# A written order for VectorE and ScalarE through the second half's short heads

## The chip, the cores and the metric

The kernel runs on one core of a Trainium2 chip. A core has a matrix engine (TensorE, PE in the profile; its weight loads are listed as PEld), an elementwise engine (VectorE, DVE), an engine for activation functions and casts (ScalarE, ACT), a general engine (GpSimd, POOL), which here mostly issues transfers, and SyncE (SP), which issues the other transfers. Each engine works through its own list of instructions in the order in which the list was built; semaphores hold an instruction until what it needs is there. The metric is the device time of one execution, in microseconds. Lower is better.

## The reference

One layer of a decoder trunk on a sequence of 1024 tokens with a model width of 2048, all in 32-bit floats:

```python
hn = rmsnorm(h, norm_mix_g[i])
proj = hn @ w_in[i]
sb_q, sb_k, sb_v, sb_g, df_q, df_k, df_v, df_g = jnp.split(proj, split_at, axis=-1)
sb_out = stick_breaking_attention(sb_q, sb_k, sb_v)          # 8 heads of 128
df_out = differential_attention(rope(df_q), rope(df_k), df_v, lam)   # 8 heads, two score maps each
df_out = rmsnorm(df_out, subln_g[i]) * (1.0 - lambda_init)
mixed = concat([sb_out * silu(sb_g), df_out * silu(df_g)])
h = h + mixed @ w_out[i]
gate = sigmoid(rmsnorm(h, norm_ple_g[i]) @ w_ple_gate[i])
h = h + gate * (p[i] @ w_ple_proj[i])
out = rmsnorm(h, norm_final_g)
```

In a stick-breaking head the weight of key s for query t is `sigmoid(z_ts)` times the product of `1 - sigmoid(z_tj)` over all j between s and t. The kernel forms that product with a scan along the keys. A differential head subtracts `lam` times a second softmax from a first one, and its output goes through a norm of its own.

## The kernel before, in words

**Three products for one.** A 32-bit product is made of three: each operand is split into a high part (a cast on ScalarE) and a low part (the rest, a subtraction on VectorE), and TensorE multiplies high by high, high by low and low by high. So nearly every tile that goes into a product costs one ScalarE instruction and one VectorE instruction first. The names end in `h` or `hi` and `l` or `lo`: `whi` and `wlo` for input weights (L149, L150), `awh` and `awl` for transposed attention weights (L375, L376).

**Halves and heads.** The tokens are worked in two halves of 512, half 1 first and then half 0. In each half come the eight differential heads (numbers 8 to 15) and then the eight stick-breaking heads (0 to 7), here called short heads, since only q and k are projected for them: their v and gate come from a stage before, by a transfer from `vg_d`. In half 0 the keys and values of half 1 are read back too (`k2`, `v2`), so a row block of 128 queries has up to 1024 keys there.

**Units and ticks.** The projection of a head is a `unit`: four pieces of weights, each two column groups of four steps. A step is three matmuls of 128 x 512 (L219 to L221), followed by one tick of a counter, `side.tick()`. A short head has one unit, 32 ticks; a differential head has two. The attention of a head does not run by itself: after its unit, `attention` returns a list of steps with tick offsets, and `side.add` mixes them into the ticks of the units that follow. So TensorE alternates between the projection of one head and the attention of the head before it. A step of offset t runs at tick t + 1. Head 7's steps run in the output stage's first products (`product(..., tick=True)`).

**The steps of a short head.** `weights(rb, c)` for the four row blocks: the scores `z` on TensorE, the causal mask (L304) on VectorE, two sigmoids (L318, L319) on ScalarE, the scan (L320) and a product (L321) on VectorE. `values` transposes v. `turn(pr, g)` transposes the weights of a pair of row blocks, and `parts` splits what comes out. `mix(pr, g)` multiplies by v (L391 to L396), and after the last group the result is summed (L401, L402), multiplied by the gate and written out by `mixed`, with transfers from SyncE (`mixed_d`, some `comb_d`) and from GpSimd (`comb_d`, added to what is there). A differential head has a softmax in place of the scan (maximum L325, exponential L328), and a norm behind its mix (`norm`, roots at L91 and L92, step at L93 to L95 and L426).

**What sets the order.** TensorE's list follows the program text throughout (`manual_schedule` over TensorE). VectorE's and ScalarE's lists follow the text only in a stage before the heads and in a part of the output stage; through the heads, the build's scheduler puts them in order. When a step runs, all of its instructions are issued at that point of the text: `weights` issues scores, mask, sigmoids, scan and product together, and the scheduler decides where they stand among the others. The eviction of q and k after a unit (L1018 to L1021) and the gate with `vf` and `gf` (L1046 to L1055) are issued directly after the unit.

**Buffers that matter here.** `z` and the transposes are in PSUM. `sg`, which holds the gate and then the output of a head, has three buffers; `sm` and `sqv` share five, `bt` has three, `qz` two. ScalarE's functions come in table sets, and where consecutive functions belong to different sets, an `ACT_TABLE_LOAD` stands between them.

Of the kernel before, what the change touches and what calls it, by code (L numbers as in the profile page):

```python
# [20 lines left out]
P = 128  # L21
# [14 lines left out]
SECOND = 16, 12  # L36
# [12 lines left out]
def _body(ctx, nc, tc, ap):  # L49
# [93 lines left out]
    def wprep(wsrc, pc, by_halves=False, later=False):  # L143
# [44 lines left out]
    class Side:  # L188

        def __init__(self):  # L190
            self.q = []
            self.now = 0

# [74 lines left out]
    def attention(at, pz, half, hd, q, qz, K, KL, VV, sg, vf):  # L268
# [10 lines left out]
        def scores(c, rb):  # L279
# [19 lines left out]
            mask = masks[:, 0 if sb else 1, :]  # L299
            if rb == 3:  # L300
                zm = ev.tile([P, P], F32, name="zm", tag="zm", bufs=1)
                V.tensor_tensor(zm, z[:, 2 * P:3 * P], mask, op=ALU.add)
                mask = zm
            V.tensor_tensor(z[:, rs], z[:, rs], mask, op=ALU.add)  # L304
            return z

        def weights(rb, c):
            off = rb * P
            vw = slice(off, nkey)
            z = scores(c, rb)  # L310
            if sb:
                pt = at.tile([P, S], F32, name="pt", tag="pt")
                if rb == 2:
                    bt = at.tile([P, S], F32, name="bt2", tag="qz")
                else:
                    bt = at.tile([P, S], F32, name="bt", tag="bt", bufs=3)
                st = at.tile([P, S], F32, name="st", tag="st")
                A.activation(pt[:, vw], z[:, vw], AF.Sigmoid, scale=-SB_SCALE)  # L318
                lastsig[0] = A.activation(bt[:, vw], z[:, vw], AF.Sigmoid, scale=SB_SCALE)  # L319
                V.tensor_tensor_scan(st[:, off + 1:nkey], pt[:, off:nkey - 1], pt[:, off:nkey - 1], initial=1.0, op0=ALU.mult, op1=ALU.bypass)  # L320
                V.tensor_tensor(bt[:, off + 1:nkey], st[:, off + 1:nkey], bt[:, off + 1:nkey], op=ALU.mult)  # L321
                ws[rb] = bt
                return
            mx = at.tile([P, 1], F32, name="mx", tag="mx", bufs=8)
            V.reduce_max(mx, z[:, vw], axis=AX.X, negate=True)  # L325
            et = at.tile([P, S], F32, name="et", tag="pt" if c else "bt", bufs=2 if c else 3)
            l = at.tile([P, 1], F32, name="l", tag="l", bufs=8)
            A.activation(et[:, vw], z[:, vw], AF.Exp, bias=mx[:, 0:1], accum_out=l)  # L328
            V.reciprocal(l, l)
            if c == 0:  # L330
                es[rb] = et, l
                return
            e0, r0 = es[rb]
            V.tensor_tensor(l, l, lam, op=ALU.mult)
            A.activation(et[:, vw], et[:, vw], AF.Copy, scale=l[:, 0:1])
            V.scalar_tensor_tensor(e0[:, vw], e0[:, vw], r0[:, 0:1], et[:, vw], op0=ALU.mult, op1=ALU.subtract)
            ws[rb] = e0

        def values():
# [5 lines left out]
            A.copy(v[:, 0], vps)  # L345
            V.tensor_tensor(v[:, 1], vps, v[:, 0].bitcast(F32), op=ALU.subtract)
            if half == 1:
                G.dma_start(v_d[hd], v.rearrange("p a b c -> p (a b c)"))
# [16 lines left out]
        def parts(pr, g, tp, wh, wl):  # L365
            if g == 0:
                lead = at.tile([P, 2, P], F32R, name="lead", tag="lead")
                A.copy(lead[:, 0], tp[:, 0, 0:P])
                V.tensor_tensor(lead[:, 1], tp[:, 0, 0:P], lead[:, 0].bitcast(F32), op=ALU.subtract)
                wjs[pr, g] = [lead, (wh[:, 1, :], wl[:, 1, :])]  # L370
                o = slice(1, 2)
            else:
                wjs[pr, g] = [(wh[:, j, :], wl[:, j, :]) for j in range(2)]
                o = slice(0, 2)
            A.copy(wh[:, o, :], tp[:, o, :])  # L375
            V.tensor_tensor(wl[:, o, :], tp[:, o, :], wh[:, o, :].bitcast(F32), op=ALU.subtract)  # L376

        def mix(pr, g):
# [22 lines left out]
            A.copy(sm[:, 1, :], av4[:, 3, :])  # L401
            V.reduce_sum(sm[:, 0, :], av4[:, 0:3, :].rearrange("p a b -> p b a"), axis=AX.X)  # L402
            av = sm.rearrange("p a b -> p (a b)")
            if sb:
                V.tensor_tensor(sg[:, ms_], av, sg[:, ms_], op=ALU.mult)
                if pr == 1:
                    mixed(half, hd, sg)
                return
            sq = ev.tile([P, 2 * P], F32, name="sqv", tag="sm", bufs=5)
            A.activation(sq, av, AF.Square)  # L410
            V.scalar_tensor_tensor(sg[:, ms_], av, subg[:, 0:1], sg[:, ms_], op0=ALU.mult, op1=ALU.mult)
            sqh = ev.tile([P, 2 * P], F32R, name="sqh", tag="sm", bufs=5)
            sql = ev.tile([P, 2 * P], F32R, name="sql", tag="sm", bufs=5)
            A.copy(sqh, sq)
            V.tensor_tensor(sql, sq, sqh.bitcast(F32), op=ALU.subtract)
            sqs[pr] = sq, sqh, sql

        def norm(pr):
# [6 lines left out]
            rstd_from(msq, 1.0, eps5, SUB_EPS, rs_, sq)  # L425
            V.tensor_tensor(sg[:, ms_], sg[:, ms_], rs_, op=ALU.mult)  # L426
            if pr == 1:
                mixed(half, hd, sg)
# [4 lines left out]
        if sb:  # L433
            b = 12 if hd == 0 else 6
            ss, t0 = [[b], [b + 3], [b + 7], [b + 11]], b + 16
            t1 = t0 + SECOND[half]
        else:
            tight = hd == 2 * H - 1
# [5 lines left out]
            t1 = s3[-1] + (13 if tight else LATD[half])  # L444
        steps = [(t, partial(weights, rb, c)) for rb, ts in enumerate(ss) for c, t in enumerate(ts)]
        steps.append((t0 - 2 if sb else ss[1][-1] + 2, values))
        for pr, t, n in ((0, t0, n0), (1, t1, n1)):
# [4 lines left out]
            steps.append((t + gap * n + (2 if sb and pr else 0), partial(mix, pr, n - 1)))  # L452
# [4 lines left out]
    with tc.tile_pool(name="at", bufs=2) as at, tc.tile_pool(name="pz", bufs=2, space=PSUM) as pz:  # L457
# [510 lines left out]
        for half in (1, 0):  # L968
# [15 lines left out]
            for hd in (ORDER0, ORDER1)[half]:  # L984
# [15 lines left out]
                acc = unit(X, mid={2: load_vg} if sb else None)  # L1000
                rstd = rstds[half]
                q = at.tile([P, 2, HALF], F32R, name="q", tag="q")
                k = at.tile([P, 2, HALF + P], F32R, name="k", tag="k")
# [9 lines left out]
                for c, t in ((0, q), (1, k)):  # L1013
                    f = f32t("qk")
                    if c == 0 and not sb:
# [3 lines left out]
                    if sb:  # L1019
                        A.copy(t[:, 0, :HALF], f)  # L1020
                        V.tensor_tensor(t[:, 1, :HALF], f, t[:, 0, :HALF].bitcast(F32), op=ALU.subtract)  # L1021
                        continue
# [23 lines left out]
                V.tensor_tensor(vf, vacc[0], rstd, op=ALU.mult)  # L1046
                V.tensor_tensor(gf, vacc[1], rstd, op=ALU.mult)
                sg = at.tile([P, HALF], F32, name="sg", tag="sg", bufs=3)
                if 0 < hd < H or (half == 0 and hd == H):
                    lastsig[0] = A.activation(sg, gf, AF.Sigmoid)  # L1050
                else:
# [518 lines left out]
```

## Time and profile before

| what | value |
| --- | --- |
| median of 3 runs | 2515.66 us (2514.49 to 2515.76) |
| profiled execution: its time, its span | 2515.73 us, 2514.0 us |
| mean granted TensorE clock | 0.991 |
| TensorE busy | 2421.5 us |
| VectorE busy | 1792.6 us |
| ScalarE busy | 1215.5 us |
| GpSimd busy | 279.6 us |
| moved by DMA | 397.72 MB |

Half 1's short heads lie at about 765 to 1060 us of the span, half 0's differential heads at 1060 to 1425, and half 0's short heads at 1425 to 1739, each unit some 36 to 38 us long but for the third, of 54 us. The output stage follows.

In the rows below, an engine's busy time counts its instructions without waiting. In a timeline row come the start, the duration, the engine, the line, the operation, output <- inputs and the tile sizes; in brackets stands how long the engine stood idle before it, and the instruction whose end released it. A matmul's duration holds its latency: what counts is the distance to the next start.

### The profile page before, as it was taken

What the parts mean: (1) busy time and instruction counts of PE and PEld (TensorE: products, weight loads), DVE (VectorE), ACT (ScalarE), POOL (GpSimd) and SP (SyncE); (2) the same over time, 40 slices, a digit from 0 to 9 for tenths busy, and PEclk for the clock granted to TensorE, in tenths of its full rate; (3) what the DMA queues carried; (4) which work ended last, traced back from release to release, by engine and by line L of the source; (5) the groups of instructions that cost most, each with busy time, mean ns of one, the idle gap of its engine ahead of it and who ended that gap; (6) DMA issues with size and microseconds to landing.
All of it is one profiled execution on the core that took longest, in us unless ns stands there. A gap on an engine that the chain in (4) does not pass through costs nothing.

```text
span 2514.0 us, 31908 instructions
## 1 busy us (share of the span) xinstructions
PE 2421.5 (96%) x11434; PEld 2005.8 (80%) x11434; DVE 1792.6 (71%) x3010; ACT 1215.5 (48%) x2067; POOL 279.6 (11%) x361
## 2 busy tenths in 40 slices
PE   8999999999999999999999988998899999999997
PEld 6787878888888887888888877887787887787886
DVE  6888777777777768688888876778577674546554
ACT  5233345555555445555566654445423224546433
POOL 1211110000000001000000000110111112330110
PEclk9999999999999999999999999999999999999998
DMA  8777654544354556343434344546746777343333
GB/s 292 255 263 223 214 193 143 164 130 151 122 153 145 168 176 186 107 113 106 122 114 122 110 122 97 143 124 186 232 162 213 169 189 230 110 137 104 131 109 101
DMA packets 167472, 397.72 MB, mean 158 GB/s; under 512 B 18897, under 2 KB 23249, under 8 KB 167313
## 3 DMA queue, kind: packets, MB, share of 16 engines
q1 hardware_dynamic: 131040, 302.07, 37.6%
q0 software_dynamic: 36272, 93.60, 14.4%
q8 instruction: 90, 1.47, 0.2%
q14 instruction: 70, 0.57, 0.1%
HBM read 297.03 MB, written 106.95 MB: 161 GB/s over the span
## 4 chain that ended last, share of the span: by engine, by line
PE 79%; DVE 10%; DMA 5%; ACT 4%; issue 3%; SPq 0%; DVEq 0%; POOL 0%; ACTq 0%
PE acc L219 16%; PE acc L220 16%; PE acc L221 16%; PE pbc L518 4%; PE pbc L516 4%; PE pbc L517 4%; PE tp L359 2%; DVE st L320 2%; PE pa L518 1%; PE pa L516 1%; PE pa L517 1%; PE av L396 1%; PE z L297 1%; PE z L298 1%; PE av L395 1%
## 5 line engine op out<-in xcount | busy, mean ns | idle before, releaser
L219 PE MATMUL acc<-xh,whi 128*128 128x512 f32 x1568 | 629.3, 401 | 1.5 <-DVE gt L1183 1.5
L221 PE MATMUL acc<-xh,wlo 128*128 128x512 f32 x1568 | 613.9, 392 | 0.0
L220 PE MATMUL acc<-xl,whi 128*128 128x512 f32 x1568 | 613.8, 391 | 0.0
L150 DVE TENSOR_TENSOR wlo<-wraw,whi 128x1024 fp32r<-128x1024 f32 x252 | 312.6, 1240 | 243.0 <-ACT whi L149 236.5
L149 ACT CAST whi<-wraw 128x1024 fp32r<-128x1024 f32 x252 | 264.9, 1051 | 295.5 <-PE acc L220 264.3
L221 PEld LDWEIGHTS acc<-xh,wlo 128*128 128x128 f32 x1568 | 295.5, 188 | 64.8
L219 PEld LDWEIGHTS acc<-xh,whi 128*128 128x128 f32 x1568 | 296.0, 189 | 57.2 <-issue 2.4
L220 PEld LDWEIGHTS acc<-xl,whi 128*128 128x128 f32 x1568 | 296.5, 189 | 54.7 <-issue 0.5
L606 ACT CAST wpr<-T 128x512 fp32r<-128x512 f32 x128 | 78.0, 621 | 317.4 <-DVE T L564 313.1
L375 ACT CAST awh<-tp 128x256 fp32r<-128x256 f32 (+1 forms) x160 | 80.1, 501 | 150.2 <-PE tp L359 124.8
L376 DVE TENSOR_TENSOR awl<-tp,awh 128x256 fp32r<-128x256 f32 (+1 forms) x160 | 92.8, 580 | 65.3 <-ACT awh L375 63.7
L328 ACT ACTIVATE et<-z,mx 128x512 f32<-128x512 f32 (+7 forms) x128 | 94.5, 738 | 51.1 <-DVE mx L325 49.5
L111 POOL TENSOR_TENSOR ssq<-ssq,sq 128x512 f32<-128x512 f32 x56 | 83.6, 1494 | 304.8 <-ACT sq L110 254.1
L320 DVE TENSOR_TENSOR_SCAN st<-pt 128x511 f32<-128x511 f32 (+3 forms) x64 | 86.5, 1352 | 23.8 <-ACT pt L318 23.8
L325 DVE TENSOR_REDUCE mx<-z 128x1 f32<-128x512 f32 (+7 forms) x128 | 96.4, 753 | 1.2
L620 DVE TENSOR_TENSOR wpr<-T,wpr 128x512 fp32r<-128x512 f32 x128 | 87.7, 685 | 5.8 <-ACT wpr L606 3.9
L396 PE MATMUL av<-awl,v 128*128 128x256 f32 x256 | 76.1, 297 | 16.0 <-DVE awl L376 15.9
L516 PE MATMUL pbc<-cS,wpr 128*128 128x512 f32 x224 | 87.4, 390 | 3.2 <-DVE u L1327 1.6
L517 PE MATMUL pbc<-cS,wpr 128*128 128x512 f32 x224 | 87.2, 389 | 0.0
L518 PE MATMUL pbc<-cS,wpr 128*128 128x512 f32 x224 | 87.2, 389 | 0.0
L318 ACT ACTIVATE pt<-z 128x512 f32<-128x512 f32 (+3 forms) x64 | 41.6, 651 | 81.6 <-DVE z L304 80.4
L394 PE MATMUL av<-awh,v 128*128 128x256 f32 x256 | 72.8, 284 | 5.5 <-ACT awh L375 5.5
(399 smaller groups left out, 5354.2 us busy)
## 6 DMA issues: line engine op xcount, KB each, us to landing
wraw<-w_in SPq DMA_DIRECT2D x192, 512.0 KB, 3.6
wraw<-w_gate SPq DMA_DIRECT2D x64, 512.0 KB, 3.6
wraw<-w_out SPq DMA_DIRECT2D x72, 256.0 KB, 3.6
wraw<-w_vg SPq DMA_DIRECT2D x71, 256.0 KB, 4.2
comb_d<-sg POOLq DMA_DIRECT2D x48, 256.0 KB, 7.5
spare<-xT SPq DMA_DIRECT2D x44, 256.0 KB, 4.2
xl<-h_d SPq DMA_DIRECT2D x40, 256.0 KB, 4.3
vghalf_d<-hc POOLq DMA_DIRECT2D x32, 256.0 KB, 4.1
```

Source lines behind the costliest of these rows:

```text
L149: A.copy(hi[:, o], raw[:, o])
L150: V.tensor_tensor(lo[:, o], raw[:, o], hi[:, o].bitcast(F32), op=ALU.subtract)
L219: T.matmul(acc[c], hi[:, k2, kh, c, :], xh, start=first, stop=False)
L220: T.matmul(acc[c], hi[:, k2, kh, c, :], xl, start=False, stop=False)
L221: T.matmul(acc[c], lo[:, k2, kh, c, :], xh, start=False, stop=last)
L320: V.tensor_tensor_scan(st[:, off + 1:nkey], pt[:, off:nkey - 1], pt[:, off:nkey - 1], initial=1.0, op0=ALU.mult, op1=ALU.bypass)
L325: V.reduce_max(mx, z[:, vw], axis=AX.X, negate=True)
L328: A.activation(et[:, vw], z[:, vw], AF.Exp, bias=mx[:, 0:1], accum_out=l)
L396: T.matmul(av, vv[:, 0, blk % 4, :], wl, start=False, stop=last)
L516: T.matmul(o, wh[:, w], xh, start=start and k == 0, stop=False, skip_group_check=True)
L517: T.matmul(o, wh[:, w], xl, start=False, stop=False, skip_group_check=True)
L518: T.matmul(o, wl[:, w], xh, start=False, stop=k == 3, skip_group_check=True)
```

## The change

The steps are cut into parts that are issued later. A new function, `side.later(dt, fn)`, runs `fn` at once as long as `side.written` is false, and dt ticks later where it is true:

```diff
+        def later(self, dt, fn):
+            if self.written:
+                self.add([(dt - 1, fn)])
+            else:
+                fn()
```

At the first short head of half 0, VectorE and ScalarE go under `manual_schedule` too, and `side.written` becomes true; both end after head 7's steps have been added, before the output stage.

```diff
+                if half == 0 and hd == 0:
+                    man3 = tc.manual_schedule(engines={V.engine, A.engine})
+                    man3.__enter__()
+                    side.written = True
...
+        side.written = False
+        man3.__exit__(None, None, None)
```

In that stretch the parts come this many ticks after their step: mask 1, sigmoids 1, scan 3, product of scan and sigmoid 5.5; maximum and exponential 1, reciprocal and scaling 3, subtraction of the two softmaxes 4.5; high parts of a turn 1, low parts 2; v 1 and 2; the sum with the gate product and `mixed` 2 (its copy 1); the norm's square 3, its low part 4, its roots 1 and its step 3 after the norm's matmul; the weights' high part 1 and low part 4 after the start of the piece before; `vf`, `gf` 5 and 6 after the unit, the gate 7, its product 10. The eviction of q and k starts at ticks 28 and 31.5 of the unit, in place of after it.

```diff
         def split(o):
-            A.copy(hi[:, o], raw[:, o])
-            V.tensor_tensor(lo[:, o], raw[:, o], hi[:, o].bitcast(F32), op=ALU.subtract)
+            side.later(1, lambda: A.copy(hi[:, o], raw[:, o]))
+            side.later(4, lambda: V.tensor_tensor(lo[:, o], raw[:, o], hi[:, o].bitcast(F32), op=ALU.subtract))
...
+                side.later(1, one)
+                side.later(3, two)
+                side.later(5.5, three)
                 return
...
+            side.later(1, high)
+            side.later(2, low)
...
+            side.later(1, roots)
+            side.later(3, step)
...
+                    if side.written:
+                        side.add([(28, partial(taken, 0)), (31.5, partial(taken, 1))])
...
+                side.later(5, partial(normed, 0, vf))
+                side.later(6, partial(normed, 1, gf))
+                side.later(7, gate)
+                side.later(10, lambda sg=sg, gf=gf: V.tensor_tensor(sg, sg, gf, op=ALU.mult))
```

The offsets of the steps change as well, for half 0's short heads and for its last differential head (`tight`):

```diff
-        if sb:
+        if sb and half == 0:
+            b = 9 if hd == 0 else 6
+            ss = [[b], [b + 8], [b + 16], [b + 24]]
+            t0, t1, tv = b + 15, b + (31 if hd == 0 else 33), b + 14
+        elif sb:
             b = 12 if hd == 0 else 6
-            ss, t0 = [[b], [b + 3], [b + 7], [b + 11]], b + 16
-            t1 = t0 + SECOND[half]
+            ss, t0, t1, tv = [[b], [b + 3], [b + 7], [b + 11]], b + 16, b + 28, b + 14
+        elif tight and half == 0:
+            ss, t0, t1, tv, gap = [[0, 2], [4, 7], [10, 13], [30, 33]], 18, 42, 9, 4
```

Here `ss` holds the ticks of the scores of the four row blocks, `t0` and `t1` the first turns of the two pairs, `tv` the values, `gap` the distance of a pair's turns. Before, half 0's short heads had `b` 6 (12 for head 0), scores at b, b + 3, b + 7 and b + 11, turns from b + 16 and b + 32, and a last mix two ticks later than now; its last differential head had [0, 1], [3, 5], [7, 9], [29, 31], values at 7, and turns from 16 and 44. For head 0 of half 0 the second row block's `bt` takes a buffer of `qz` too. Half 1's short heads keep their offsets; their parts are issued at once, though some in another order of the text, which the scheduler then orders.

More of the change, by code (lines that the diff above doesn't have):

```diff
@@ L35 @@
 GAPS, GAPD = 4, 6
-SECOND = 16, 12
 PRIO = 300
@@ new lines, in two, with three @@
+            def two():
+                et, l = es[rb, c]
+                V.reciprocal(l, l)
+                if c:
+                    V.tensor_tensor(l, l, lam, op=ALU.mult)
+                    A.activation(et[:, vw], et[:, vw], AF.Copy, scale=l[:, 0:1])
+            def three():
+                et, l = es[rb, 1]
+                e0, r0 = es[rb, 0]
+                V.scalar_tensor_tensor(e0[:, vw], e0[:, vw], r0[:, 0:1], et[:, vw], op0=ALU.mult, op1=ALU.subtract)
+                ws[rb] = e0
@@ L339, in values @@
+            side.later(1, one)
+            side.later(3, two)
+            if c:
+                side.later(4.5, three)
         def values():
@@ L344, in values, with low @@
             v = at.tile([P, 2, 4, P], F32R, name="v", tag="v")
[L345 to L348, printed above, removed]
+            side.later(1, lambda: A.copy(v[:, 0], vps))
+            def low():
+                V.tensor_tensor(v[:, 1], vps, v[:, 0].bitcast(F32), op=ALU.subtract)
+                if half == 1:
+                    G.dma_start(v_d[hd], v.rearrange("p a b c -> p (a b c)"))
+            side.later(2, low)
             VV.insert(0, v)
@@ L451, in attention @@
                 steps.append((t + gap * g, partial(turn, pr, g)))
-            steps.append((t + gap * n + (2 if sb and pr else 0), partial(mix, pr, n - 1)))
+            steps.append((t + gap * n + (2 if sb and half and pr else 0), partial(mix, pr, n - 1)))
             if not sb:
```

185 lines of the change are left out of this document (112 added, 73 removed).

## The prediction

> **What bounds the kernel now.** I read the page first, then the busy time by window, then TensorE's idle time by what ended it, then the single stalls in the timeline.
>
> ```profile
> span 2514.0 us, 31908 instructions
> PE 2421.5 (96%) x11434; PEld 2005.8 (80%) x11434; DVE 1792.6 (71%) x3010; ACT 1215.5 (48%) x2067; POOL 279.6 (11%) x361
> ```
>
> TensorE is the bound, and its instructions are the same in both kernels, so the change can only move the stretches in which it waits (92.5 us in all) or runs slowly. The next rows are windows of before (start:end, length, then busy us and count of PE, PEld, DVE, ACT, POOL, then the granted clock, DMA share, GB/s). The first is the sum over half 1's short heads (765 to 1060 us), the second half 0's differential heads; the next eight are, one unit each, half 0's short heads 0 to 7; the last two are the output stage's start.
>
> ```profile
> sum 295.00, PE 287.00 PEld 238.80 DVE 217.78 ACT 147.45 POOL 18.37; mean PE 71.75 PEld 59.70 DVE 54.44 ACT 36.86 POOL 4.59
> 1060.00:1425.00 365.00, 365.00 (x1846) 309.27 (x1845) 294.22 (x551) 213.37 (x366) 25.20 (x35) 1.00 0.43 119
> 1425.00:1461.00 36.00, 35.09 (x182) 29.21 (x181) 28.87 (x53) 23.07 (x39) 3.21 (x4) 1.00 0.45 119
> 1461.00:1498.00 37.00, 33.95 (x164) 27.94 (x163) 29.67 (x46) 24.19 (x38) 1.63 (x3) 0.95 0.32 103
> 1498.00:1552.00 54.00, 43.13 (x218) 35.85 (x217) 32.64 (x48) 24.06 (x36) 6.39 (x8) 0.94 0.41 99
> 1552.00:1589.00 37.00, 34.90 (x188) 29.45 (x187) 27.48 (x38) 16.48 (x27) 3.75 (x5) 1.00 0.53 139
> 1589.00:1626.00 37.00, 35.67 (x192) 30.25 (x191) 28.51 (x40) 17.37 (x28) 3.74 (x5) 1.00 0.47 129
> 1626.00:1662.00 36.00, 34.67 (x188) 29.43 (x187) 27.57 (x38) 16.38 (x28) 3.76 (x5) 1.00 0.46 125
> 1662.00:1700.00 38.00, 36.68 (x196) 31.06 (x195) 29.38 (x40) 18.02 (x29) 3.74 (x5) 1.00 0.50 136
> 1700.00:1739.00 39.00, 34.94 (x186) 29.21 (x185) 34.08 (x51) 23.36 (x39) 3.16 (x4) 1.00 0.66 182
> 1739.00:1800.00 61.00, 55.58 (x285) 45.89 (x284) 39.45 (x55) 33.16 (x57) 5.80 (x9) 0.97 0.63 195
> 1800.00:1860.00 60.00, 54.56 (x235) 44.22 (x234) 36.55 (x59) 16.87 (x31) 8.31 (x14) 0.97 0.65 206
> ```
>
> TensorE's idle time over the eight units is 0.9 + 3.1 + 10.9 + 2.1 + 1.3 + 1.3 + 1.3 + 4.1 = 25.0 us; in the output stage's first 121 us another 10.9. So 25 us is nearly all that this edit can reach. VectorE is at 75 to 87% of each window without being the bound: what counts is which of its instructions stands in front.
>
> The stalls themselves (start, duration, what, idle before and its releaser):
>
> ```profile
> 1483.27 0.39 PE L394 MATMUL av<-awh,v 128*128 128x256 f32 x1 [1.29 <-ACT awh L375]
> 1485.48 0.39 PE L396 MATMUL av<-awl,v 128*128 128x256 f32 x1 [1.71 <-DVE awl L376]
> 1487.25 0.63 PE L221 MATMUL acc<-xh,wlo 128*128 128x512 f32 x1
> 1487.68 0.63 PE L219 MATMUL acc<-xh,whi 128*128 128x512 f32 x1
> 1503.98 1.12 PE L359 MATMUL tp<-ident,bt 128*128 128x128 f32 x4 [3.45 <-DVE sqv L93]
> 1521.26 0.39 PE L394 MATMUL av<-awh,v 128*128 128x256 f32 x1 [2.00 <-ACT awh L375]
> 1524.10 0.57 PE L396 MATMUL av<-awl,v 128*128 128x256 f32 x1 [2.34 <-DVE awl L376]
> 1538.62 0.44 PE L343 MATMUL vps<-ident,vf 128*128 128x128 f32 x2 [2.22 <-DVE awl L376]
> 1616.79 0.40 PE L220 MATMUL acc<-xl,whi 128*128 128x512 f32 x1
> 1617.03 0.40 PE L221 MATMUL acc<-xh,wlo 128*128 128x512 f32 x1
> 1643.84 0.38 PE L396 MATMUL av<-awl,v 128*128 128x256 f32 x1 [1.09 <-DVE awl L376]
> ```
>
> The 3.0 us of 1483 to 1485 are followed by matmuls 0.43 us apart (1487.25 to 1487.68) where 0.24 is usual (1616.79 to 1617.03). The windows show this as a granted clock of 0.95 and 0.94: about 0.05 x 37 + 0.06 x 54 = 5.1 us by those rounded shares. I take 4.5, so the stage loses 29.5 us. The 1.09 us stall of a steady head has no such tail (clock 1.00 there).
>
> **The change part by part.** No instruction of TensorE, VectorE, SyncE or GpSimd is added or removed. The order of VectorE and ScalarE over half 0's short heads becomes the written one.
>
> *The gate (L1046 to L1055), now 5 to 10 ticks after the unit.* In before, a gate is put into ScalarE's order early, and it blocks:
>
> ```profile
> 1507.38 0.88 POOL L260 DMA_DIRECT2D comb_d<-sg  x1 [13.93 <-DVE sg L426]
> 1516.03 1.28 ACT L1050 ACT_TABLE_LOAD   x1 [5.42 <-DMA comb_d<-sg]
> 1517.33 0.63 ACT L1050 ACTIVATE sg<-gf 128x512 f32<-128x512 f32 x1
> ```
>
> It waits for the transfers of head 15 to free an `sg` buffer (three are held), and the sigmoids and high parts of the current head wait behind it on ScalarE for 5.4 us. Of the 10.9 idle us of 1498 to 1552, 2.00, 2.34 and 2.22 above go back to this. Written, this gate comes seven ticks after its unit, at least 20 us after 1516: the block goes whole. What is late next there is the ordinary stall of a steady head (below).
>
> *The norm's roots (L91, L92), together at +1, the step at +3.* Before:
>
> ```profile
> 1499.47 1.28 ACT L91 ACT_TABLE_LOAD   x1
> 1501.76 1.28 ACT L92 ACT_TABLE_LOAD   x1
> 1503.05 0.42 ACT L92 ACTIVATE rsub<-rsub 128x256 f32<-128x256 f32 x1
> 1503.50 0.43 DVE L93 SCALAR_TENSOR_TENSOR sqv<-msq,rsub 128x256 f32<-128x256 f32 x1 [1.03 <-ACT rsub L92]
> ```
>
> Two table loads and a cast of `k` between them hold the transposes of head 0 for 3.45 us. In the changed order the next transposes are written three ticks (2.1 us) and some attention products later, and the cast no longer stands between: I take 0.6 of the 3.45, bounds 0 and 3.45. Three table loads fewer (3 x 1.28 = 3.8 us) lie on ScalarE, which has 13 us or more to spare in every unit: nothing.
>
> *The steady heads: weights every eight ticks instead of three or four, lows two ticks after the turn, the scan at +3.* A tick is three matmuls, 3 x 0.23 = 0.7 us. One place binds in the changed order: the first mix of the second pair of a head, written at tick 12 of the next unit. Its low part (L376) is written behind scan 0 of the new head, whose scores end at tick 7. Durations from 1552 to 1700 (grouped, busy and mean ns):
>
> ```profile
> L320 DVE TENSOR_TENSOR_SCAN st<-pt 128x1023 f32<-128x1023 f32 x4 | 9.1, 2282 | 0.0
> L318 ACT ACTIVATE pt<-z 128x1024 f32<-128x1024 f32 x4 | 4.1, 1020 | 0.0
> L304 DVE TENSOR_TENSOR z<-z,masks 128x128 f32<-128x128 f32 x12 | 3.4, 284 | 0.0
> L369 DVE TENSOR_TENSOR lead<-tp,lead 128x128 fp32r<-128x128 f32 x8 | 2.3, 282 | 0.0
> L376 DVE TENSOR_TENSOR awl<-tp,awh 128x256 fp32r<-128x256 f32 x8 | 3.4, 421 | 0.4
> ```
>
> From the end of the scores: 0.28 + 1.02 + 2.28 + 0.28 + 0.42 = 4.3 us to the low part. TensorE has four ticks and a turn of three transposes meanwhile, 2.8 + 0.3 = 3.1. So it waits 1.2 us in every unit. The windows of heads 3 to 6 show 1.3 to 2.1 today, for the same kind of reason (the 1.09 of 1643.84): nothing gained in a steady head, and 0.5 in all. The weight parts `whi`, `wlo`, now +1 and +4, are needed at +8: hidden by four ticks.
>
> *The last differential head (weights [0,2], [4,7], [10,13], [30,33]) and its tail.* Its sequels now stand in one line with those of head 0. In head 0's unit the first mix of head 15 waits behind a maximum, an exponential, a scaling and the subtraction of the third block, none of which it needs: bounds 0.9 (today's idle) and 3.45 (the longest stall of the stage); I take the upper, since VectorE has 28.9 of 36 us to do there. In head 1's unit, the second pair's first low part stands behind scan 0, 2.28 us: I take 2.3. The 3.0 with their slow matmuls go.
>
> *Head 7's unit.* Its idle 4.1 comes with VectorE at 34 of 39 us, as operands of the output stage are split between the heads' instructions. They still are: I leave 4.0.
>
> *The output stage's start.* One thing is worse: head 6's last scores come at tick 31 of that unit instead of 18, so their sigmoids come behind casts that wait for a transfer:
>
> ```profile
> 1742.86 0.62 ACT L504 CAST cS4h<-cS4l 128x512 fp32r<-128x512 f32 x1 [4.00 <-DMA cS4l<-comb_d]
> ```
>
> Bounds 0 and 4.0; I take 1.0.
>
> *Half 1's short heads.* Only the place of a few instructions moves; idle there is 295 - 287 = 8 us, so -3 to +3, taken as 0.
>
> *Transfers.* The mixed output and with it GpSimd's three `comb_d` issues come one or two ticks later. GpSimd is busy 3.8 us of 37, and the loads of `k2`, `v2` behind them are needed half a unit later: 0. SyncE's `mixed_d` issue is as late; the next weights (`wraw`) queue behind it, covered by the two buffers of a piece each (eight ticks, 5.6 us): 0, and 1.4 a unit if that cover is gone.
>
> *Sum.* After: 3.5 + 2.3 + (1.2 + 0.6) + 4 x 1.2 + 4.0 = 16.4 idle, plus 1.6 for slow matmuls behind the 3.5 (eight, 0.2 each) = 18.0, against 29.5: -11.5; the tail +1.0: -10.5. The profiled execution took 2515.73 us (span 2514.0), 0.07 over the median, so 2505.2.
>
> **The rivals.**
> (1) *More goes.* If the written order keeps head 15's products and head 7's unit as tight as the steady ones, all eight units idle 1.2 and none is slow: 9.6 instead of 29.5, about 2496. For it: from 1060 to 1425, with longer chains and the same VectorE share, TensorE is never idle. Against it: 2.28 us scans in a fixed line.
> (2) *Nothing net.* A fixed line makes every wait a wait for all behind it. At 1.3 us more in each of the eight units the gain is used up: 2515. For it: VectorE is at 75% or more, so a late instruction is caught up slowly.
> (3) *Slower.* The binding place is 1.2 us long by my chain, and the stalls that were 1.7 to 3.5 long are followed by slow matmuls. If a unit's stall grows past about 2.2 (one 0.7 us gate product and handovers between the engines in the chain), each costs 1.0 + 1.6 more; in seven units +18, so about 2523. It turns the sign from 10.5 / 7 = 1.5 us more a unit. For it: handovers aren't in my sums. Against it: the 1.09 stall today has none of that tail.
> [...]
>
> **How the numbers follow.** Forecast (-5 to -17) 0.42; rival 1 (beyond -17) 0.17; rival 2 (within 0.2%, 5 us, about what can be told from no change) 0.16; rival 3, or another loss over 5 us, 0.25. Faster is 0.42 + 0.17 = 0.59. The range goes from 2490 (rival 1 with half of the output stage's idle) to 2524 (rival 3), and holds 0.8; the forecast's own is 2499 to 2511.
>
> **What would show it.** Right: no ScalarE row at L1050's new place waiting for `comb_d`; no stall over 1.5 us between the third and the seventh short head's unit; one wait of about 1.2 us a unit, TensorE for the 256-wide low part behind a 1023-long scan; clock 1.00 from head 1 on; heads about 36.5 us apart. Wrong: a repeated stall over 2 us, a unit longer than 37.5 us, new waits of the weights (`wraw`) for their transfers, or the output stage's idle above 14 us.

## The result, and the profile after

The changed kernel takes 2491.77 us (median of 4 runs, 2487.77 to 2494.21) against 2515.07 us (2512.03 to 2515.76) for the kernel before on the same chip: a ratio of 0.9908, with a 95% interval of 0.9891 to 0.9925. That is 23.3 us, where 10.5 were forecast. The sign was right, the size was not. The profiled execution took 2487.77 us, the lowest of the four.

The page of the changed kernel, first lines:

```profile
span 2486.0 us, 31946 instructions
PE 2404.7 (97%) x11434; PEld 1997.5 (80%) x11434; DVE 1794.5 (72%) x3010; ACT 1207.2 (49%) x2064; POOL 279.3 (11%) x361
```

TensorE's count of instructions is the same, but its busy time fell by 16.8 us, more than its idle time, which went from 92.5 to 81.3. An estimate from the mean granted clock of the two profiles, 0.991 and 0.994, puts 0.009 x 2514 - 0.006 x 2486 = 7.7 us of it down to fewer slow matmuls. The rest, 9.1 us by that estimate, is put down to waiting that the profile counts as busy; the experiments show 0.13 us of it in front of one product. Part of the surprise lies there, and the next section takes it apart.

The windows of the changed kernel, one for each unit of half 0's short heads 0 to 7 (start:end, length, then busy us and count of PE, PEld, DVE, ACT, POOL, then granted clock, DMA share, GB/s):

```profile
1422.50:1459.00 36.50, 32.91 (x166) 27.88 (x165) 25.85 (x46) 17.76 (x32) 3.22 (x4) 0.95 0.42 108
1459.00:1495.40 36.40, 33.03 (x165) 27.39 (x163) 28.25 (x45) 22.45 (x39) 1.11 (x2) 0.95 0.30 94
1495.40:1532.80 37.40, 37.28 (x205) 31.91 (x206) 31.22 (x44) 21.16 (x33) 6.40 (x8) 1.00 0.62 155
1532.80:1568.20 35.40, 34.90 (x190) 29.80 (x189) 28.39 (x38) 16.66 (x28) 3.75 (x5) 1.00 0.52 136
1568.20:1603.70 35.50, 34.99 (x191) 29.81 (x190) 28.43 (x39) 16.73 (x28) 3.77 (x5) 1.00 0.50 133
1603.70:1639.10 35.40, 34.88 (x190) 29.80 (x189) 28.39 (x38) 16.79 (x28) 3.76 (x5) 1.00 0.52 135
1639.10:1674.50 35.40, 34.88 (x190) 29.79 (x189) 28.38 (x39) 16.67 (x28) 3.75 (x5) 1.00 0.50 133
1674.50:1717.80 43.30, 37.57 (x199) 31.36 (x199) 37.94 (x56) 23.77 (x41) 3.75 (x5) 1.00 0.65 192
```

TensorE's idle time, unit by unit, is 3.6 + 3.4 + 0.1 + 0.5 + 0.5 + 0.5 + 0.5 + 5.7 = 14.8 us, where 25.0 stood before and 16.4 were forecast. The unit of 54 us has become one of 37.4. The last unit is worse than it was: 5.7 us idle in a window of 43.3, where 4.1 stood in one of 39. The clock is 0.95 in the first two units.

The stalls in the timeline of the changed kernel (start, duration, what, idle before and releaser):

```profile
1447.06 0.47 PE L440 MATMUL av<-lead,v 128*128 128x256 f32 x2 [3.59 <-DVE awl L422]
1475.11 0.80 PE L440 MATMUL av<-lead,v 128*128 128x256 f32 x2 [2.00 <-DVE lead L421]
1582.30 0.51 PE L440 MATMUL av<-lead,v 128*128 128x256 f32 x2 [0.51 <-DVE lead L421]
1691.71 0.51 PE L440 MATMUL av<-lead,v 128*128 128x256 f32 x2 [3.46 <-DVE lead L421]
```

Three stand where the prediction put them: the first mix of head 15 (3.5 forecast), its second pair behind head 0's scan (2.3), and, as in the third row, once in each steady head behind the 1023-long scan (1.2). The fourth, 3.46 us in head 7's unit, was not forecast.

To compare stages across kernels I use a mark that every kernel has in the same place of TensorE's order, the start of each head's transposes of v (`vps`). The table gives the time between such marks in the profiled execution, in us. "Half 1" runs from the last differential head of half 1 to the first of half 0 and so holds half 1's short heads; "heads 14 to 1" holds the step from the differential heads to the short ones; S2 is the output stage's first product with `cS2h`, and the last column ends with TensorE's last product.

| kernel | half 1 | differential, to 14 | 14 to 1 | 1 to 5 (four heads) | 5 to 6 | 6 to 7 | 7 to S2 | S2 to the end |
| --- | --- | --- | --- | --- | --- | --- | --- | --- |
| before | 285.9 | 350.7 | 159.1 | 148.8 | 37.5 | 44.5 | 40.1 | 691.3 |
| changed | 280.2 | 350.6 | 147.7 | 141.8 | 39.1 | 43.9 | 41.7 | 685.0 |
| changed, once more | 279.9 | 350.7 | 148.9 | 142.0 | 41.7 | 46.2 | 41.9 | 690.8 |

So the gain has three places: half 1's short heads (-5.7), which the prediction set at nothing; the step to the short heads (-11.4, and -10.2 in the second profile), which it had; and the four heads from 1 to 5 (-7.0), of which it had 0.5. Of these 7.0, 3.2 lie between heads 1 and 2 (38.62 to 35.46), where the kernel before isn't steady yet; 0.7 of them is work that only moved, since six products of 0.12 us stand ahead of head 1's mark in the changed kernel and behind it in the kernel before. The three heads that follow gain 1.3 each. From head 5 to S2 the changed kernel loses 2.6, and 7.7 in its second profile. The -6.3 after S2 isn't the change's: the second profile of the same kernel shows -0.5 there.

### The profile page after: what moved, and what is told of

Its sections match the earlier page's. It is cut to its first block, busy times and chain, and to the rows that moved or that the text cites. A ratio compares the mean times of both kernels' runs of the same rounds, so it can differ in the third digit from the quotient of the medians.

```text
span 2486.0 us, 31946 instructions
## 1 busy us (share of the span) xinstructions
PE 2404.7 (97%) x11434; PEld 1997.5 (80%) x11434; DVE 1794.5 (72%) x3010; ACT 1207.2 (49%) x2064; POOL 279.3 (11%) x361
## 4 chain that ended last, share of the span: by engine, by line
PE 81%; DVE 8%; DMA 5%; ACT 4%; issue 3%; SPq 0%; DVEq 0%; ACTq 0%
PE acc L226 16%; PE acc L227 16%; PE acc L228 16%; PE pbc L598 4%; PE pbc L596 4%; PE pbc L597 4%; PE tp L398 2%; PE pa L596 1%; PE pa L598 1%; PE pa L597 1%; PE z L305 1%; PE z L304 1%; PE av L445 1%; PE av L444 1%; PE av L443 1%
## 5 line engine op out<-in xcount | busy, mean ns | idle before, releaser
L422 DVE TENSOR_TENSOR awl<-tp,awh 128x256 fp32r<-128x256 f32 (+1 forms) x160 | 92.3, 577 | 31.5 <-ACT awh L417 30.7
L328 ACT ACTIVATE pt<-z 128x512 f32<-128x512 f32 (+3 forms) x64 | 41.7, 651 | 89.6 <-DVE z L312 81.1
L226 PE MATMUL acc<-cA11h,whi 128*128 128x512 f32 x192 | 76.2, 397 | 0.6 <-DVE qk L1092 0.6
```

Of the source, the lines that this page charges most:

```text
L226: T.matmul(acc[c], hi[:, k2, kh, c, :], xh, start=first, stop=False)
```

## The experiments

**What shortened half 1.** Half 1's steps keep their offsets, and its order isn't written. Besides the place where some buffers are taken, q's and k's among them, one thing in the text differs for it: `high` casts `lead` and `awh`, and `low` then issues both low parts, where before the low part of `lead` came between the two casts. Two kernels take this apart: the old kernel with the new text order, and the changed kernel with the old one.

```diff
 (parts_only, to the kernel before)
             A.copy(lead[:, 0], tp[:, 0, 0:P])
-            V.tensor_tensor(lead[:, 1], tp[:, 0, 0:P], lead[:, 0].bitcast(F32), op=ALU.subtract)
...
         A.copy(wh[:, o, :], tp[:, o, :])
+        if g == 0:
+            V.tensor_tensor(lead[:, 1], tp[:, 0, 0:P], lead[:, 0].bitcast(F32), op=ALU.subtract)
         V.tensor_tensor(wl[:, o, :], tp[:, o, :], wh[:, o, :].bitcast(F32), op=ALU.subtract)
```

> The kernel before, with one thing changed for all heads: in `parts`, the low part of `lead` is issued after the cast of `awh` and no longer before it. TensorE's order is the same. Theory A (half 1's short heads became 5.7 us shorter in the changed kernel because this text order moves `awl` ahead of other instructions in the scheduled order): 2515 - 5 = 2510 us, steady short heads of half 1 27.25 us apart in place of 27.5. Rival B (those 5.7 us are chance or come from something else, as the place where q and k get their buffers): 2514 to 2516 us and 27.5 us.

```diff
 (half1_old, to the changed kernel)
+            if not side.written:
+                if g == 0:
+                    A.copy(lead[:, 0], tp[:, 0, 0:P])
+                    V.tensor_tensor(lead[:, 1], tp[:, 0, 0:P], lead[:, 0].bitcast(F32), op=ALU.subtract)
+                A.copy(wh[:, o, :], tp[:, o, :])
+                V.tensor_tensor(wl[:, o, :], tp[:, o, :], wh[:, o, :].bitcast(F32), op=ALU.subtract)
+                return
             side.later(1, high)
             side.later(2, low)
```

> The changed kernel with the old text order of `parts` wherever the order is not written (half 1's short heads and all differential heads but the last ones). Theory A: it loses half 1's share, 2492 + 5.5 = 2497 us, half 1's heads 27.5 us apart. Rival B: 2491 to 2493 us.

Measured: parts_only 0.9961 (0.9945 to 0.9976), 2504.8 us; half1_old 0.9934 (0.9916 to 0.9952), 2499.2 us. Half 1 took 278.9 us in parts_only (27.26 a head) and 286.8 in half1_old (27.51). Theory A holds: the one text order takes the time from half 1 and, put back, returns it. In the old kernel two lines in another order are worth about 10 us of 2515 (6 to 14 by the interval), where 5 were expected. Half 1 gained 7.0 there and the step from 14 to 1 another 2.0 (157.1 in place of 159.1). Heads 1 to 5 of half 0 gained nothing: the last three take 36.46 us each in place of 36.71, but the first takes 39.85 in place of 38.62.

The mechanism can be read in one head of half 1. VectorE and TensorE in the kernel before:

```profile
842.28 1.23 DVE L150 TENSOR_TENSOR wlo<-wraw,whi 128x1024 fp32r<-128x1024 f32 x1 [0.96 <-ACT whi L149]
843.42 0.42 DVE L376 TENSOR_TENSOR awl<-tp,awh 128x256 fp32r<-128x256 f32 x1
843.64 0.28 PE L395 MATMUL av<-awh,v 128*128 128x256 f32 x1
843.89 0.39 PE L396 MATMUL av<-awl,v 128*128 128x256 f32 x1
```

and the same place in the changed kernel:

```profile
840.75 0.41 DVE L422 TENSOR_TENSOR awl<-tp,awh 128x256 fp32r<-128x256 f32 x1
841.52 1.23 DVE L149 TENSOR_TENSOR wlo<-wraw,whi 128x1024 fp32r<-128x1024 f32 x1 [0.35 <-ACT whi L148]
842.88 0.28 PE L444 MATMUL av<-awh,v 128*128 128x256 f32 x1
843.00 0.28 PE L445 MATMUL av<-awl,v 128*128 128x256 f32 x1
```

Before, `awl` stands behind the 1.23 us `wlo`, ends at 843.84, and TensorE's next product starts 0.25 us after the one before it, and the instruction behind it another 0.23 later; in the changed kernel `awl` stands first and both distances are 0.12. The wait of 0.13 us isn't shown as idle in either view, because the product before it (0.28 long with its latency) is still counted as running. The windows of one such head, before and changed:

```profile
838.38:865.89 27.51, 27.51 (x138) 23.06 (x137) 19.60 (x35) 12.14 (x25) 1.23 (x2) 1.00 0.52 172
```

```profile
837.62:864.88 27.26, 27.26 (x139) 23.03 (x138) 19.79 (x35) 11.95 (x25) 1.23 (x2) 1.00 0.54 174
```

TensorE is busy all the time in both, with the same work (a record is missing in places), and yet one is 0.25 us shorter, of which the two distances are 0.24. Such waits, the visible ones at half 1's two ends (8.0 us of idle before, 5.9 after, in 765 to 1060) and a few slow matmuls at 959 us of the kernel before (0.43 us apart, 959.63 to 960.06) make up the 5.7; their shares were not measured one by one.

**The gate.** The kernel before, with the gates held behind the cast of k:

```diff
 (gate_after_k, to the kernel before)
-                        A.copy(t[:, 0, :HALF], f)
+                        kcast = A.copy(t[:, 0, :HALF], f)
...
+                if half == 0 and 0 < hd < H:
+                    with tc.issue_after(kcast.ins):
+                        lastsig[0] = A.activation(sg, gf, AF.Sigmoid)
-                if 0 < hd < H or (half == 0 and hd == H):
+                elif 0 < hd < H or (half == 0 and hd == H):
                     lastsig[0] = A.activation(sg, gf, AF.Sigmoid)
```

> The kernel before, with the gates of half 0's short heads 1 to 7 held behind the cast of k of the same head on ScalarE, nothing else. Theory G (head 2's gate, placed early, blocks ScalarE while head 15's transfers run, and stalls of 2.00, 2.34 and 2.22 us with slow matmuls hang on it): these go, 2515 - 8 = 2507 us. Rival (the stalls of that unit have other causes, or another wait ends as late): 2513 to 2516 us.

Measured: 0.9976 (0.9966 to 0.9985), 2507.6 us; 14 to 1 took 152.0 in place of 159.1. Theory G holds in its sum. Two of its parts were wrong, and this shows what was left (stalls of gate_after_k):

```profile
1507.08 1.11 PE L359 MATMUL tp<-ident,bt 128*128 128x128 f32 x4 [5.39 <-DVE sqv L93]
1536.22 0.66 PE L343 MATMUL vps<-ident,vf 128*128 128x128 f32 x4 [2.06 <-DVE awl L376]
```

The 2.22 us stall at `vps` is still there with 2.06: it didn't hang on the gate. And the norm's stall grew from 3.45 to 5.39, because head 1's gate, with a third table load (1.28 us each in the kernel before), now stood between the two roots. What went were the 2.00 and 2.34 in head 2's unit and the 3.0 with their slow matmuls in head 1's. The run moved two gates in this stretch, though: head 2's sigmoid from 1517.33 to 1550.37, and head 1's from 1467.78, where it had a table load of its own and two more for head 15's roots behind it (at 1466.49, 1470.10 and 1471.89, 1.28 us each), to 1504.21. The 3.0 us of 1483 to 1485 lie before head 2's gate, so they can't hang on it; that they hang on head 1's is likely, but no run moves one gate alone.

**Both small edits, and no written order.**

> The kernel before with two small edits and no written order: the text order in `parts` (as in parts_only) and the gates of half 0's heads 1 to 7 held behind the cast of k (as in gate_after_k). Theory: the two touch different places and add up, 2515 - 10 - 7.6 = 2497.5 us, so that the written order with its spread is worth another 6 us, all in half 0's steady heads. Rival: the two share a gain, 2500 to 2505 us.

Measured beside the changed kernel on one chip: two_edits 0.9924 (0.9909 to 0.9940), 2496.0 us; the changed kernel 0.9914 (0.9896 to 0.9932), 2496.4 us. The two edits add up, as the theory had it (2497.5). The further 6 us that it left to the written order aren't there on this chip. Against the changed kernel two_edits has the same half 1 (280.5) and the same 14 to 1 (148.9), loses the steady heads (148.4 in place of 142.0), and wins from head 5 to S2 (121.7 in place of 129.8 here, 124.7 in the first profile). In whole runs the two can't be told apart.

> The changed kernel itself once more, as the level for the three beside it: 2489 to 2495 us by every theory.

**Order or offsets.** The new offsets without the written order, and the written order with the scores six ticks apart (`ss = [[b], [b + 6], [b + 12], [b + 18]]`):

```diff
 (offsets_only, to the changed kernel)
-                if half == 0 and hd == 0:
-                    man3 = tc.manual_schedule(engines={V.engine, A.engine})
-                    man3.__enter__()
-                    side.written = True
...
-        side.written = False
-        man3.__exit__(None, None, None)
```

> The changed kernel without the written order: all new step offsets and the spread of the last differential head, but every sequel is issued with its step and the scheduler orders VectorE and ScalarE. Theory W (the written order removes the blocks and makes the steady heads shorter): half 1's 5 us stay, of the rest at most a third, 2505 to 2510 us, steady heads above 36.2 us. Rival O (the wider spacing of the scores does it): 2491 to 2496 us, steady heads at 35.5 us.

> The changed kernel with the scores of half 0's short heads six ticks apart in place of eight. Theory: in a written line the spacing has to leave VectorE room for scan and product between two scores; at six ticks (4.2 us of TensorE's own work) 1023-long and 895-long scans with their products still fit, but the low parts of the turns come behind them: heads 36.0 us apart in place of 35.4, 2492 + 4 = 2496 us. Rival: the spacing is not what counts, 2490 to 2494 us.

Measured: offsets_only 1.0047 (1.0033 to 1.0061), 2526.4 us, slower than before; spaced_6 0.9918 (0.9904 to 0.9931), 2494.6 us. A steady head of each, and one of the kernel before and of the changed one, in windows from mark to mark, in the order before, changed, offsets_only, spaced_6:

```profile
1577.24:1613.93 36.69, 35.36 (x191) 30.00 (x190) 28.21 (x38) 17.07 (x28) 3.75 (x5) 1.00 0.47 129
```

```profile
1557.31:1592.78 35.47, 34.96 (x190) 29.81 (x189) 28.43 (x39) 16.70 (x27) 3.75 (x6) 1.00 0.50 134
```

```profile
1570.51:1611.74 41.23, 37.04 (x190) 31.24 (x189) 28.86 (x39) 16.93 (x27) 3.76 (x6) 0.96 0.43 115
```

```profile
1598.83:1634.76 35.93, 35.21 (x190) 29.71 (x190) 28.40 (x39) 17.04 (x27) 3.78 (x5) 1.00 0.51 133
```

Both theories of offsets_only fell: I expected a smaller gain, and it was a loss of 11 us. The scheduler, given the same offsets, puts the low parts of a turn behind the scan, the scan's product and a `wlo`, 4.2 us idle in each head, and the first of these stalls (2.68 us) is followed by matmuls 0.43 us apart; the clock of that window is 0.96. The written order is what makes the new offsets bearable. The spacing itself is worth 0.45 us a head (35.92 against 35.47): the theory's direction with most of its 0.6, but in the whole run too little to be seen, so the rival is what the times say. The old offsets under the written order were not tried: on paper they block each other's buffers.

**The last differential head.** The changed kernel with this head's old offsets (tight_old), and with its turns from 21 and 43 (tight_21):

```diff
 (tight_old, to the changed kernel)
-        elif tight and half == 0:
-            ss, t0, t1, tv, gap = [[0, 2], [4, 7], [10, 13], [30, 33]], 18, 42, 9, 4
```

> The changed kernel with the last differential head's old offsets in half 0 (scores [0,1], [3,5], [7,9], [29,31], values 7, turns from 16 and 44), everything else written as in the changed kernel. Theory: its scores come closer together than VectorE's written line can follow, the stall of 3.6 us at its first mix grows and slow matmuls follow: 2491.8 + 3 = 2495 us. Rival: the line is set by what follows, and the spread is worth nothing: 2490 to 2493 us.

> The changed kernel with the last differential head's turns three and one ticks later (first pair from 21, second from 43). Theory: the first mix no longer waits 3.6 us for its low part behind the third block's softmax: 2491.8 - 3.6 - 0.8 of slow matmuls + 0.5 = 2488 us. Rival: the mixes, pushed into head 1's unit, meet head 0's scan there, and the wait moves: 2491 to 2494 us.

Measured: tight_old 0.9934 (0.9921 to 0.9948), 2496.8 us; tight_21 0.9914 (0.9901 to 0.9928), 2491.4 us. In the marks neither differs: 14 to 1 took 147.8 in both, 147.7 and 148.9 in the changed kernel. In tight_old the 3.6 us stall is gone and 2.5 us for `wlo`, 1.9 for `sql` and 2.5 for `sqv` stand in its place; in tight_21 several waits of 0.2 to 2.1 us stand there. For tight_21 the rival was right. For tight_old the marks speak for the rival, but the time of 2496.8 is near the theory's 2495. The profiled execution, 2492.6 us, was the fastest of its five, so its marks can't say what the slower ones lost. That this stretch has a fixed amount of waiting, and that moving one head's steps only says which instruction shows it, fits both profiles; whether the spread is worth something in whole time stays open.

**The stalls that are left.** `hold_a11` holds the output stage's first casts on ScalarE; `scan_later` issues the scan 3.5 ticks after the scores; `scan0_hold` does the first and, for the first row block only, the second (`leads` lists the casts of `lead` in their order):

```diff
 (hold_a11, scan0_hold, to the changed kernel)
-        for i in range(4):
-            operand(0, "A11", i)
+        with tc.issue_after(leads[-2].ins):
+            for i in range(4):
+                operand(0, "A11", i)
...
 (scan0_hold)
-                side.later(3, two)
+                side.later(3 if rb else 3.5, two)
```

> The changed kernel with the four casts of the output stage's first operand (`cA11h`) held on ScalarE behind the cast of `lead` of head 5's second pair. In the changed kernel the first of them waits 3.8 us for its transfer and head 6's first sigmoids wait behind it; TensorE then waits 3.5 us at head 5's mix. Theory: that wait shrinks to 0.5 us as in the units before: 2491.8 - 3 - 0.7 = 2488 us. Rival: the same work comes later in that unit or at the output stage's start and stalls there: 2491 to 2493 us.

> The changed kernel with the scan issued 3.5 in place of 3 ticks after the scores, so that the low parts of the same tick stand ahead of it on VectorE. Theory: the 0.5 us wait for `lead` behind the 1023-long scan goes in head 3's to head 6's unit, and the 2.0 us wait in head 1's: 2491.8 - 4 - 0.7 of slow matmuls = 2487 us, heads 35.0 us apart. Rival: the scan, 0.7 to 1.4 us later, makes its product and the next turn late, and a wait of the same size stands there: 2491 to 2493 us, heads 35.4 us apart.

> The changed kernel with the first operand's casts held (as in hold_a11) and the scan of the first row block alone at 3.5 ticks, behind the low parts of its tick. Theory: the 0.5 us wait of each steady head goes, and since the other scans stay where they are, nothing else becomes late; the 2.0 us in head 1's unit go to 1.2: 2488.9 - 4 x 0.5 - 2.4 = 2484.5 us, heads 34.9 us apart. Rival: the first product comes later and the sum of the pair before with it, a wait of 0.5 us or more in its place: 2488 to 2491 us.

Measured: hold_a11 0.9902 (0.9888 to 0.9915), 2488.9 us; scan_later 0.9947 (0.9935 to 0.9960), 2500.2 us, slower than the changed kernel; scan0_hold 0.9892 (0.9879 to 0.9906), 2488.3 us, where the changed kernel had 2496.4 on the same chip.

For hold_a11 the local theory is right in the main. ScalarE in the changed kernel:

```profile
1683.46 0.62 ACT L584 CAST cA11h<-cA11l 128x512 fp32r<-128x512 f32 x1 [3.82 <-DMA cA11l<-mixed_d]
1687.61 0.62 ACT L584 CAST cA11h<-cA11l 128x512 fp32r<-128x512 f32 x1 [1.48 <-DMA cA11l<-mixed_d]
1688.13 1.02 ACT L328 ACTIVATE pt<-z 128x1024 f32<-128x1024 f32 x1
```

and in hold_a11, with what TensorE then waits:

```profile
1686.52 1.03 ACT L329 ACTIVATE pt<-z 128x1024 f32<-128x1024 f32 x1 [1.30 <-DVE z L313]
1689.69 2.21 ACT L585 CAST cA11h<-cA11l 128x512 fp32r<-128x512 f32 x4
1690.10 0.51 PE L441 MATMUL av<-lead,v 128*128 128x256 f32 x2 [1.55 <-DVE lead L422]
```

The four casts no longer wait, the sigmoid starts as soon as its scores are there, and the 3.46 shrink to 1.55, where 0.5 was expected. From head 5 to S2 the gain is 0.4 by the marks against the first profile (124.3 against 124.7) and 5.5 against the second (129.8); in the whole time it can't be told from nothing.

In scan_later the rival's mechanism was right, and the loss larger than either theory had. The 0.5 us wait shrank to 0.17, and this one came, in every head:

```profile
1594.40 0.55 PE L398 MATMUL tp<-ident,bt 128*128 128x128 f32 x3 [1.18 <-DVE sm L454]
```

The later scans push back their products and the sum behind them, and the next head's turn waits for that sum: 37.17 us a head in place of 35.45. With only the first scan moved, a steady head has no wait left (scan0_hold):

```profile
1589.00:1623.87 34.87, 34.87 (x190) 29.80 (x189) 28.23 (x40) 16.72 (x28) 3.78 (x5) 1.00 0.51 136
```

34.87 us a head where 34.9 were expected (35.43 in hold_a11, which has the same casts held), and 145.4 in place of 148.9 from 14 to 1. The whole time is the rival's all the same, 2488.3 and not 2484.5: from head 5 to S2 it took 127.8, with a new stall of 2.27 us. This version beats the kernel before clearly and the changed one on the same chip (2486.7 to 2489.3 against 2489.2 to 2499.8); against the changed kernel's first runs, 2487.8 to 2494.2 on another chip, the lead is 3.5 us.

## Why the prediction was right and wrong

Two terms of the sum failed, half 1 (taken as 0) and the steady heads (nothing gained), and they have a reason in common: what the kernel before loses to waits was read from TensorE's idle time alone. In the steady heads the wait left after the change was also put too long. By the marks the sum was 1.2 us or less off in the step to the short heads, 5.7 off in half 1 and about 6 off in the steady heads, and too kind by 1.6 or more from head 5 to S2.

*The gate:* right that it blocks, and that the block goes with the written order. The price by stalls was partly wrong: the `vps` stall was put on its account and isn't its.

*The norm's roots:* 0.6 was taken, 0.1 of idle is left in that unit. Right.

*Head 15 and its tail:* 3.5 and 2.3 forecast, 3.59 and 2.00 measured, in the places named. The whole stretch of the first three units was forecast to go from 19.4 us lost to 9.2; the marks show -11.4 and -10.2 against these -10.2. Right, but for the clock: it was to be 1.00 from head 1 on, and head 1's window shows 0.95, since slow matmuls (0.42 us apart) followed the 2.00 us stall too, where the sum has them behind the 3.5 alone.

*The steady heads* ("nothing gained in a steady head, and 0.5 in all"): wrong, 7.0 us over four heads. The 0.5 doesn't fit the sum either, whose terms for these units go from 6.0 to 4.8. The wait that was to bind is there, but 0.5 us long and not 1.2:

```profile
1577.63 0.39 PE L302 MATMUL z<-k,q 128*128 128x512 f32 x1
1578.39 0.29 DVE L312 TENSOR_TENSOR z<-z,masks 128x128 f32<-128x128 f32 x1
1579.77 2.29 DVE L335 TENSOR_TENSOR_SCAN st<-pt 128x1023 f32<-128x1023 f32 x1 [0.50 <-ACT pt L328]
1581.98 0.27 DVE L421 TENSOR_TENSOR lead<-tp,lead 128x128 fp32r<-128x128 f32 x1
1582.16 0.41 DVE L422 TENSOR_TENSOR awl<-tp,awh 128x256 fp32r<-128x256 f32 x1
```

The mix's first products need only `lead` and the high parts, and `awl` is made beside them, so its 0.42 doesn't belong to the chain. From the scores' end (1578.02) to that of `lead` (1582.25) are 4.2 us, nearly the 4.3 of the prediction with `awl`, as the mask comes 0.37 late. But TensorE has five ticks and the transposes meanwhile, 3.8 us up to 1581.79, and not four ticks and 3.1. The before side was read from idle time alone, 1.33 us a head. The windows show 36.69 to 35.47 us, of which 0.82 is idle and 0.40 lies in TensorE's busy time. A spacing shorter than the product's listed duration is no idle time in the profile (the 0.25 us behind 843.64, with 0.28 listed), and the written order removed some of these as well. The first of the four, from head 1 to 2, was not yet steady before: it gave 3.2 of the 7.0, and no run takes these 3.2 apart.

*Half 1* ("taken as 0", -3 to +3): wrong, -5.7. The argument was that only the place of a few instructions moves and that 8 us of idle bound it. The bound was read from a view that doesn't show the waits in question, and the moved instruction was the one that TensorE waits for. parts_only shows this part alone.

*Head 7's unit and the output stage* (4.0 idle left, +1.0): the loss has the right sign, the size is 2.6 and 7.7 by the marks of the two profiles. The 3.46 us stall stands in head 7's unit and not in the output stage: there the first casts for the output stage wait for a transfer with head 6's first sigmoids behind them, and hold_a11 shows this for the stall. It doesn't show that the stage's loss hangs on it, and that stays open. The unit's window of 43.3 us is also past the 37.5 that was to be a sign of being wrong, though it was 39 before.

*One reading:* VectorE was said to be at 75 to 87% of each window; in the third it is at 60% (32.64 of 54). No term uses it.

*The rivals.* A gain beyond 17 had a chance of 0.17. The time is nearest to rival 1's 2496, by another way: not every unit is down to 1.2, and half 1 isn't in that rival. Rival 3 didn't happen in the changed kernel, but offsets_only is a picture of it, 2.7 us of stall in each head with slow matmuls behind it.

## What to carry to other kernels

Time lost on the bounding engine is read from the distance between the starts of its instructions, and compared with the same instructions where nothing waits; idle time left out waits like the 0.13 us behind a product listed at 0.28. In an order that a scheduler makes, look for the short instruction that the bounding engine waits for next and for what stands before it: here two lines in another order brought about 10 us, and the hold of a few early gates, one of which waited 5.42 us for a transfer in front of others, 7.6. These two small edits together brought as much as the whole written order with its offsets (2496.0 and 2496.4 us). A written order is worth having where its steps are placed by what waits for them; half a tick on all scans cost about 8 us, and the same half tick on the first scan alone took the last wait out of every steady head.

## What the runs showed of the hardware

The length of a stall didn't decide alone whether slow matmuls followed. In the changed kernel the 2.00 us stall of 1475.11 is followed by them, and the 3.46 us stall of 1691.71 isn't:

```profile
1477.63 0.63 PE L227 MATMUL acc<-xl,whi 128*128 128x512 f32 x1
1478.05 0.61 PE L228 MATMUL acc<-xh,wlo 128*128 128x512 f32 x1
...
1693.32 0.40 PE L228 MATMUL acc<-xh,wlo 128*128 128x512 f32 x1
1693.56 0.40 PE L226 MATMUL acc<-xh,whi 128*128 128x512 f32 x1
```

0.42 us apart in the first pair, 0.24 in the second. The second profile of the same kernel has the same stall in the same place, and there it is followed by them, 0.43 apart:

```profile
1692.85 0.79 PE L440 MATMUL av<-lead,v 128*128 128x256 f32 x2 [3.46 <-DVE lead L421]
1695.79 0.63 PE L228 MATMUL acc<-xh,wlo 128*128 128x512 f32 x1
1696.22 0.63 PE L226 MATMUL acc<-xh,whi 128*128 128x512 f32 x1
```

The 2.68 of offsets_only has them too (0.43 apart), and so has a 1.70 of the kernel before (1744.47, with 0.53 more before 1745.73; 0.43 apart from 1746.12 on), while the longer 2.22 of the kernel before (1538.62) is followed by matmuls 0.23 apart (1539.58 to 1539.81). So the prediction's rule, slow matmuls behind stalls of 1.7 us and more, is too simple; what decides was not shown.

The stage from S2 to TensorE's last product took 685 to 692 us in the profiles of all these kernels, though nothing in its text differs, and 685.0 and 690.8 in two profiles of the same kernel. Most of that difference is again slow matmuls: by the records the first has 10 of the size 128x512 there at the slow spacing, the second 28, at about 0.2 us more each (0.43 apart where 0.23 is usual), 3.6 of the 5.8 us. The whole time goes with the granted clock in the same way: of the five executions in after_again the two at 0.993 and 0.994 took 2489.2 and 2491.2 us, the two at 0.990 took 2499.8 and 2498.0. What decides in a given execution isn't known; it is why effects under 5 us are read here from marks and not from whole times.
